# Dilated attention: the steps that merge the three groups moved to other places, and a later load of token differences

## The chip, the cores and the metric

The kernel runs on one core of one Trainium2 chip. The metric is the device time of one execution in microseconds. A core has five engines that each work through their own list of instructions strictly in order: TensorE (PE in the profile, with PEld for loading its stationary operand), VectorE (DVE), ScalarE (ACT), GpSimd (POOL) and SyncE (SP), which in this kernel only issues DMA transfers. Engines wait for each other by semaphores. PE writes to eight PSUM banks; everything else is held in on-chip memory (SBUF) or in device memory.

## The reference, cut to what matters

The whole kernel is one encoder block with three parallel mixers, gates, and two projections. The change concerns the first mixer, attention over three groups of dilated windows, whose outputs are merged with softmax weights over the groups:

```python
for gi, (window, dil) in enumerate(A_GROUPS):          # (128, 1), (512, 4), (2048, 16)
    hs = slice(gi * A_HEADS, (gi + 1) * A_HEADS)       # 8 heads of 64 in each group
    o_g, lse_g = dilated_window_attention(aq[:, :, hs], ak[:, :, hs], av[:, :, hs], window, dil)
    outs.append(o_g)
    lses.append(lse_g)
wts = jax.nn.softmax(jnp.stack(lses, axis=0), axis=0).astype(dt)
oa = jnp.einsum('gbsh,gbshd->bshd', wts, jnp.stack(outs, axis=0)).reshape(b, s, BRANCH_WIDTH)
```

Everything is float32, with 1024 tokens and a width of 1024. Dense products are done with each operand split into a high part (fp32r) and a remainder, and three products (high by high, low by high, high by low).

## The kernel before, in words

**Stages.** The kernel goes through stages one after the other. The change touches dilated attention (about 735 to 1010 us of the profiled span), and the first microseconds of the next stage, which computes gate products with a blocked scheme of seven products (`PRODUCTS`) and needs differences of token blocks ("T2", "T3", "T1", "T4") that an earlier stage left in device memory (`tsd`).

**Items.** Dilated attention is cut into twelve items `(p_, g)`: four pairs of heads, and for each pair the groups 0, 1 and 2. `seq` lists them, in the order (0,0), (0,1), (0,2), (1,0) and so on. `item` (line 1276) returns the pieces of one item for eight token tiles T = 0 to 7:

- `scores(b)`: PE multiplies queries and keys for four token tiles into four PSUM banks (`pss1`, four buffers).
- `soft(T)`: for each of two heads DVE adds the mask and takes the row minimum (L1355), and ACT takes the exponential with a row sum (L1356).
- `trans(T)`: PE transposes the probabilities (L1373, L1382) into a PSUM bank (`pst`, two buffers), and ACT copies them to `app` (L1385).
- `pv(b)`: PE multiplies four tiles' probabilities with the values (L1399) into a bank of the same two-buffer kind, and ACT copies the result to `og` (L1407).
- `stats`: row minima and sums are transposed and written to device memory (`std`).

**The plan.** `plan` (line 1448) lines up the pieces of one item with the tail of the item before it and the head of the next. In each step T stand, in this order: `stats` of the item before (T = 2), `soft(T)`, the merge steps that are due (`combining(T)`), in the last item the token differences (`tokens(T)`), keys for an item two further on (`keys`: in T = 1 a fetch by SP, in T = 5 `k_add`, two additions on POOL, L1274), then `trans(T - 2)` (for T below 2: `trans(T + 6)` of the item before). T = 3 ends with `pv(1)` of the item before joined with `scores(1)` of this one, and T = 7 with `pv(0)` of this one joined with `scores(0)` of the next. `values` (SP loads) follow these two. So `trans(4)` and `trans(5)` come just ahead of `pv(0)`, and `trans(6)`, `trans(7)` are done in the next item.

**Weaving.** `weave` (line 176) mixes these pieces, by their planned cost, with one dense unit for each item: 48 matmuls of 512 columns into two `d` banks, whose results DVE and POOL rotate into the queries `aq` of the item two further on (L1207, L1210, L1211), taken from a list `pend`. In the second half of a unit the next unit's weights are split (`a_split`: ACT `wh`, then DVE `wl`, L105 and L106). In the items (3,1) and (3,2) the units are gates instead (one unit and three units). On DVE, ACT, POOL and SP the order is the order in which the code runs; nothing is reordered later.

**Merging the groups.** When the third group's `pv(1)` of pair p is done (T = 3 of item (p+1, 0)), `ready` puts the steps of `combine` (line 1508) into the list `todo`, and `combining(T)` runs a step when T equals the entry of `STEP_T` (line 1594) that belongs to it. For pairs 0 to 2 the steps are:

- `fetch`: SP loads minima and sums of the three groups from `std` to `cpt` (two DMAs).
- `weights`: seven small DVE operations and a reciprocal, with one ACT exponential between them, give the weights `ceg`.
- `put`: SP writes them to device memory (`wgd`, two DMAs).
- `get`: SP loads them back, spread over 64 partitions each, as three tiles `wgt` (six DMAs of 256 KB).
- three times `weigh(g)`: DVE multiplies `og` of group g by its weights (L1551, 128x1024), and for g = 1, 2 POOL adds it to group 0 (L1553).
- `store`: SP writes the sum to `od`.

Pair 3 is merged in the next stage from a table of its own (`COM`), which the change doesn't touch.

**The last item.** In front of item (3,2) the tiles `wgt` (three), `kraw`, `kswp`, `t1a`, `aq`, `ak` are reused for token differences: eight loads of 256 KB (`load_block`, SP), which are split on ACT and DVE (`split_block`) two at a time in T = 2 to 5 (`tokens`). The tail of that item (`plan(None, ...)`, T = 0 to 3: `trans(6)`, `trans(7)`, `stats`, `pv(1)`) follows, and then the next stage begins with the products A11·B11, A12·B21 and S2·T2.

Of the kernel before, what the change touches and what calls it, by code (L numbers as in the profile page):

```python
# [9 lines left out]
R = mybir.dt.float32r  # L10
# [5 lines left out]
S = 1024  # L16
NT = 8
P = 128
# [32 lines left out]
def block(ctx: ExitStack, tc: tile.TileContext, x, xT, memT, cst, msk, bcst, tabA, gpost,  # L51
# [52 lines left out]
    def split(dst_h, dst_l, src):  # L104
        A.activation(dst_h, src, AF.Copy)  # L105
        V.tensor_tensor(dst_l, src, dst_h.bitcast(F32), op=OP.subtract)  # L106
# [136 lines left out]
    def pool(name, side="left"):  # L243
        p = tc.tile_pool(name=name, bufs=1, side=side, reuse_waits="tile")
        return p, p.__enter__()
# [109 lines left out]
    late = []  # L355
# [823 lines left out]
    abp, ab = pool("ab")  # L1179
    with tc.tile_pool(name="aa", bufs=1, reuse_waits="tile") as aa:  # L1180
# [263 lines left out]
        def joined(*pieces):  # L1444
            pieces = [x for x in pieces if x]
            return (lambda: [fn() for fn, _ in pieces]), JOINED

        def plan(it, pre, nxt):

            out = []  # L1450

            def combining(T):
                while todo and T == STEP_T[-len(todo)]:
                    todo.pop(0)()

            def tokens(T):
                if T >= 2:
                    for nm, k in late[:2]:
                        split_block(nm, k)
                    del late[:2]  # L1460
                if T == 5:
                    token_tiles("T1", [ab.tile([P, S], R, name=f"a{c}", bufs=2) for c in "qk"])
                    load_block("T1", (0, 1))

            def keys(key, T):
                (k_fetch if T == 1 else k_add)(*key)

            def ready():
                if pre and pre["key"][1] == 2:
                    todo.extend(combine(pre["key"][0], [OG.pop((pre["key"][0], x)) for x in range(3)]))  # L1470

            if it and not pre:
                out.append(it["scores"][0])
            for T in range(NT if it else 4):
                if T == 2 and pre:
                    out.append(pre["stats"])
                if it:
                    out.append(it["soft"][T])
                out.append((lambda T=T: combining(T), 0.0))
                if it and not nxt:  # L1480
                    out.append((lambda T=T: tokens(T), 0.0))
                if it and it["ahead"] and T in (1, 5):
                    out.append((lambda T=T: keys(it["ahead"], T), 0.0))
                if T < 2:
                    if pre:
                        out.append(pre["trans"][T + 6])
                elif it:
                    out.append(it["trans"][T - 2])
                if T == 3:
                    out.append(joined(pre and pre["pv"][1], it and it["scores"][1]))  # L1490
                    if it:
                        out.append(it["values"][1])
                    if pre and it:
                        out.append((ready, 0.0))
                if T == 7:
                    out.append(joined(it["pv"][0], nxt and nxt["scores"][0]))
                    if nxt:
                        out.append(nxt["values"][0])
            return out

        def run(pieces):
            for fn, cost in pieces:
                yield cost
                fn()

        OG = {}

        def combine(p_, ogs):

            c = {}  # L1510
            wgt = [None] * 3

            def load(g):
                wgt[g] = (ab if p_ < 3 else cb).tile([P, S], F32, name="wgt", bufs=3 if p_ < 3 else 1)
                for h in range(2):
                    nc.sync.dma_start(wgt[g][h * 64:h * 64 + 64], wgd[p_, h, g:g + 1].to_broadcast([64, S]))

            def fetch():
                c["t"] = cb.tile([P, 3, 2, 16], F32, name="cpt", bufs=1)
                for h in range(2):  # L1520
                    nc.sync.dma_start(c["t"][h * 64:h * 64 + 64], std[p_, h].rearrange("g s (i e) -> i g s e", e=16))

            def weights():
                cpt = c["t"]
                mn = cb.tile([P, 16], F32, name="cmn", bufs=2)
                V.tensor_tensor(mn, cpt[:, 0, 0], cpt[:, 1, 0], op=OP.min)
                V.tensor_tensor(mn, mn, cpt[:, 2, 0], op=OP.min)
                eg = cb.tile([P, 3, 16], F32, name="ceg", bufs=1)
                V.tensor_tensor(eg, cpt[:, :, 0], mn[:, None, :].to_broadcast([P, 3, 16]), op=OP.subtract)
                A.activation(eg, eg, AF.Exp, scale=-1.0)  # L1530
                dn = cb.tile([P, 3, 16], F32, name="cdn", bufs=1)
                V.tensor_tensor(dn, eg, cpt[:, :, 1], op=OP.mult)
                ds_ = cb.tile([P, 16], F32, name="cds", bufs=2)
                V.tensor_tensor(ds_, dn[:, 0], dn[:, 1], op=OP.add)
                V.tensor_tensor(ds_, ds_, dn[:, 2], op=OP.add)
                V.reciprocal(ds_, ds_)
                V.tensor_tensor(eg, eg, ds_[:, None, :].to_broadcast([P, 3, 16]), op=OP.mult)
                c["e"] = eg

            def put():  # L1540
                for h in range(2):
                    nc.sync.dma_start(wgd[p_, h].rearrange("g (i e) -> i g e", e=16), c["e"][h * 64:h * 64 + 64])

            def get():
                for g in range(3):
                    load(g)

            def weigh(g):
                wv = wgt[g].rearrange("p (b a) -> p a b", b=16)
                ogv = ogs[g].rearrange("p (a b) -> p a b", b=16)  # L1550
                V.tensor_tensor(ogv, ogv, wv, op=OP.mult)  # L1551
                if g:
                    G.tensor_tensor(ogs[0], ogs[0], ogs[g], op=OP.add)  # L1553

            def store():
                nc.sync.dma_start(od[0, p_], ogs[0])

            w3 = [lambda g=g: weigh(g) for g in range(3)]
            if p_ < 3:
                return [fetch, weights, put, get] + w3 + [store]  # L1560
            return [fetch, weights, put] + [f for g in range(3) for f in (lambda g=g: load(g), w3[g])] + [store]
# [16 lines left out]
        TB = {}  # L1578

        def token_tiles(nm, tiles):  # L1580
            TB.setdefault(nm, []).extend([t[:, half[x]] for x in range(2)] for t in tiles)

        def load_block(nm, ks=range(4)):
            for k in ks:
                nc.sync.dma_start(TB[nm][k][1].bitcast(F32), tsd[int(nm[1]) - 1, k])

        def split_block(nm, k):
            h, l = TB[nm][k]
            split(h, l, l.bitcast(F32))

        late = []

        todo = []
        STEP_T = (4, 7, 7, 0, 3, 5, 7, 2)
        seq = [(p_, g) for p_ in range(4) for g in range(3)]
        counter = iter(range(len(AU)))
        add_a(*seq[0])
# [18 lines left out]
        for n in range(len(seq)):  # L1616
            if n + 2 < len(seq):
                add_a(*seq[n + 2])
            elif n + 2 == len(seq):
                for j in GATES_A:  # L1620
                    add_ag(*j)
            last = n + 1 == len(seq)
            if last:
                token_tiles("T2", [ab.tile([P, S], R, name="wgt", bufs=3) for k in range(3)])
                token_tiles("T2", [ab.tile([P, S], R, name="kraw")])
                token_tiles("T3", [ab.tile([P, S], R, name="kswp")])
                TB["T3"].append([ab.tile([P, 512], R, name="t1a", bufs=2) for _ in range(2)])
                token_tiles("T3", [ab.tile([P, S], R, name=f"a{c}", bufs=2) for c in "qk"])
                load_block("T2")
                load_block("T3")  # L1630
                late += [("T2", k) for k in range(4)] + [("T3", k) for k in range(4)]
            pieces = plan(items[n], items[n - 1] if n else None, items[n + 1])
            if last:
                pieces += plan(None, items[n], None)
            weave(len(GATES_A) - 1 if last else 1, run(pieces), sum(c for _, c in pieces), 1.0)
# [20 lines left out]
    last = len(pairs) - 1  # L1656
# [82 lines left out]
    steps = [(n, i, f) for n, i in enumerate((2, 0, 1)) for f in range(8)]  # L1739
# [13 lines left out]
    pre = {}  # L1753
# [163 lines left out]
    for T in range(NT):  # L1917
# [7 lines left out]
        for a, b in cuts:  # L1925
            c = slice(a, b)
# [21 lines left out]
        else:  # L1948
# [9 lines left out]
            for h, (a, b) in enumerate(cuts):  # L1958
                c = slice(a, b)
# [131 lines left out]
```

## Time and profile before

| | us |
|---|---|
| runs, median (lowest, highest) | 1453.93 (1451.42, 1454.14) |
| the profiled execution, its own time | 1452.82 |
| the profiled execution, span from first to last instruction | 1450.8 |
| dilated attention within the span | about 735 to 1010 |
| granted TensorE clock, mean over the span | 0.993 |

The rows shown further down come from views of this one profiled execution. A row of the timeline has the start in us from the span's start, the duration in us, the engine, the line of the kernel and the operation, its output and input tiles, shapes, and how many equal instructions follow each other (x); a bracket gives the idle time of the engine before it and what ended it. A row of the busy-time table has the stretch, its length, and the busy time and number of instructions of PE, PEld, DVE, ACT and POOL, then the granted clock of PE (1.00 is full speed), the share of the DMA engines and GB/s. A row of the waits has who waited, for whom, the total in us, how many times, and the longest.

### The profile page before, as it was taken

The numbers are of one execution on the slowest core, as the hardware profiler recorded it, in microseconds if no ns is written. First come the engines' busy times: TensorE is split into PE (matmuls) and PEld (weight loads), VectorE is DVE, ScalarE is ACT, GpSimd is POOL, SyncE is SP. The second block draws the span as 40 slices with busy tenths as digits, with TensorE's granted clock in tenths as the row PEclk, the third lists the DMA queues.
The fourth block names the chain that finished last, engine by engine and source line by source line (L and its number), as shares of the span: only waits on it lengthen the run. The fifth ranks groups of instructions, "written<-read, shape, count | busy, mean of one in ns | idle before, by whom it ended". The sixth has DMA issues, their size and how long they took to land.

```text
span 1450.8 us, 21207 instructions
## 1 busy us (share of the span) xinstructions
PE 1412.4 (97%) x7556; PEld 1137.8 (78%) x7556; DVE 996.3 (69%) x1765; ACT 656.9 (45%) x1423; POOL 507.4 (35%) x390
## 2 busy tenths in 40 slices
PE   8999999999999999999999898989999999999998
PEld 7899986565666888888888777877787887888887
DVE  7765468776763884788866767655877787559643
ACT  6544365665654453322166475646443344223221
POOL 1415504666664001433244343411333331044322
PEclk9999999999999999999999999999999999999999
DMA  6332012232112788444634546363444443767122
GB/s 238 102 117 74 20 62 91 81 105 74 56 50 88 250 264 280 141 167 167 193 95 120 120 117 153 85 174 104 151 135 140 172 175 130 260 212 272 55 88 102
DMA packets 114137, 198.68 MB, mean 137 GB/s; under 512 B 24624, under 2 KB 55408, under 8 KB 114032
## 3 DMA queue, kind: packets, MB, share of 16 engines
q1 hardware_dynamic: 87824, 166.75, 36.4%
q10 hardware_dynamic: 26208, 30.58, 6.0%
q8 instruction: 59, 0.97, 0.3%
q14 instruction: 46, 0.38, 0.1%
HBM read 142.40 MB, written 54.89 MB: 136 GB/s over the span
## 4 chain that ended last, share of the span: by engine, by line
PE 76%; DVE 8%; ACT 5%; issue 4%; DMA 4%; POOL 3%; ACTq 0%; SPq 0%; POOLq 0%; DVEq 0%
PE s L125 16%; PE sc L125 9%; PE d L145 6%; PE d L143 6%; PE d L147 6%; PE s L1059 5%; PE sc L1937 5%; PE ov L761 3%; PE s L1343 2%; PE tr L1399 2%; PE s L745 2%; PE tr L727 2%; PE s L746 2%; PE d L542 2%; PE d L1059 1%
## 5 line engine op out<-in xcount | busy, mean ns | idle before, releaser
L143 PE MATMUL d<-hh,wh 128*128 128x512 f32 x480 | 195.8, 408 | 1.6 <-DVE fth L228 1.6
L147 PE MATMUL d<-hh,wl 128*128 128x512 f32 x480 | 193.6, 403 | 0.0
L145 PE MATMUL d<-hl,wh 128*128 128x512 f32 x480 | 191.8, 400 | 0.0
L752 POOL TENSOR_TENSOR bl<-bl,bp 128x512 f32<-128x512 f32 x96 | 131.4, 1369 | 53.7 <-ACT bp L748 48.2
L105 ACT ACTIVATE wh<-wr 128x512 fp32r<-128x512 f32 (+1 forms) x91 | 68.8, 772 | 141.7 <-PE sc L125 78.4
L125 PE MATMUL sc<-hh,wh 128*128 128x512 f32 x384 | 118.5, 390 | 2.2 <-ACT rs L1694 2.2
L1356 ACT ACTIVATE pra<-pra,sts 128x192 f32<-128x192 f32 (+2 forms) x192 | 84.6, 442 | 76.0 <-DVE sts L1355 75.6
L106 DVE TENSOR_TENSOR wl<-wr,wh 128x512 fp32r<-128x512 f32 (+1 forms) x63 | 77.3, 1245 | 58.2 <-ACT wh L105 58.0
L143 PEld LDWEIGHTS d<-hh,wh 128*128 128x128 f32 x480 | 90.6, 189 | 22.9 <-issue 4.0
L145 PEld LDWEIGHTS d<-hl,wh 128*128 128x128 f32 x480 | 90.6, 189 | 22.3 <-issue 6.5
L147 PEld LDWEIGHTS d<-hh,wl 128*128 128x128 f32 x480 | 90.6, 189 | 21.5 <-issue 4.5
L728 DVE TENSOR_REDUCE bn<-tr 128x1 f32<-128x512 f32 x128 | 86.1, 685 | 17.8 <-PE tr L727 16.4
L748 ACT ACTIVATE bp<-s 128x512 f32<-128x512 f32 x128 | 75.8, 595 | 47.0 <-PE s L746 46.1
L106 DVE TENSOR_TENSOR ch<-sf,ch 128x512 fp32r<-128x512 f32 x68 | 57.9, 852 | 44.5 <-ACT ch L105 44.5
L125 PEld LDWEIGHTS sc<-hh,wh 128*128 128x128 f32 x384 | 72.1, 188 | 17.4 <-issue 2.6
L1664 POOL TENSOR_TENSOR sf<-wr 128x512 f32<-128x512 f32 x22 | 32.0, 1474 | 151.6 <-DVE ch L106 59.5
L105 ACT ACTIVATE ch<-sf 128x512 fp32r<-128x512 f32 x68 | 41.6, 628 | 90.0 <-PE s L125 46.4
L1207 DVE SCALAR_TENSOR_TENSOR t2a<-d,tab 32x512 f32<-32x512 f32 x96 | 66.0, 687 | 22.7 <-PE d L147 20.7
L1868 POOL TENSOR_TENSOR acc<-acc,th 128x1024 f32<-128x1024 f32 x15 | 40.6, 2708 | 111.8 <-DVE th L1867 111.8
L997 POOL TENSOR_TENSOR sf<-wr 128x512 f32<-128x512 f32 x12 | 19.0, 1583 | 167.2 <-DMA wr<-in_wu 109.6
L1211 POOL TENSOR_TENSOR aq<-t1a,t2a 128x512 f32<-128x512 f32 x24 | 45.4, 1893 | 86.8 <-DVE t1a L1210 86.8
L125 PE MATMUL sc<-hl,wh 128*128 128x512 f32 x192 | 74.8, 389 | 0.0
(392 smaller groups left out, 3773.1 us busy)
## 6 DMA issues: line engine op xcount, KB each, us to landing
wr<-in_wu SPq DMA_DIRECT2D x64, 512.0 KB
kd<-kr ACTq DMA_DIRECT2D x48, 256.0 KB
th<-thd SPq DMA_DIRECT2D x24, 512.0 KB
thd<-rs ACTq DMA_DIRECT2D x44, 256.0 KB
g2d<-fth SPq DMA_DIRECT2D x24, 256.0 KB
kraw<-kd SPq DMA_DIRECT2D x12, 512.0 KB
kswp<-kd SPq DMA_DIRECT2D x48, 128.0 KB
wgt<-wgd SPq DMA_DIRECT2D x24, 256.0 KB
```

The source lines that it names most:

```text
L105: A.activation(dst_h, src, AF.Copy)
L106: V.tensor_tensor(dst_l, src, dst_h.bitcast(F32), op=OP.subtract)
L125: PE.matmul(out_ps, a, b, start=i == 0, stop=i == n - 1)
L143: PE.matmul(dst, wh[:, k, :], hh[k][:, t], start=k == 0, stop=False)
L145: PE.matmul(dst, wh[:, k, :], hl[k][:, t], start=False, stop=False)
L147: PE.matmul(dst, wl[:, k, :], hh[k][:, t], start=False, stop=k == 7)
L728: fp["last"] = V.tensor_reduce(st[i]["n"][:, j, c:c + 1], s, axis=AX.X, op=OP.min)
L748: A.activation(pp, s, AF.Exp, scale=-1.0)
L752: G.tensor_tensor(lsum[i % 2], lsum[i % 2], pp, op=OP.add)
L1059: PE.matmul(now[j], a, b, start=k == 0 and q == 0, stop=k == end and q == 2)
L1356: A.activation(src, src, AF.Exp, scale=-1.0, bias=bias, accum_out=sts[:, h, 1, T:T + 1])
L1937: PE.matmul(parts[h], *terms[h][j], start=j == 0, stop=j == 23)
```

## The change

Four things change, all in the stage of dilated attention.

1. `fetch` is no longer in `todo`: it runs at once in `ready` (end of T = 3 of item (p+1, 0)).
2. The other seven steps get new places. Before: `weights` and `put` in T = 7 of item (p+1, 0); `get` in T = 0 and the three `weigh` in T = 3, 5, 7 of item (p+1, 1); `store` in T = 2 of item (p+1, 2). Now: `weights` in T = 5, `put` in T = 6, `get` in T = 7 of item (p+1, 0); `weigh(0)` and `weigh(1)` in T = 4 and 5 of item (p+1, 1); `weigh(2)` in T = 4 and `store` in T = 7 of item (p+1, 2).
3. The tiles for the token differences T2 and T3 are taken and loaded in T = 4 of the last item instead of in front of it.
4. They are split in T = 6 and 7 of the last item and in the first two steps of its tail (two in each), instead of in T = 2 to 5.

```diff
             def tokens(T):
-                if T >= 2:
-                    for nm, k in late[:2]:
-                        split_block(nm, k)
-                    del late[:2]
+                if T == 4:
+                    token_tiles("T2", [ab.tile([P, S], R, name="wgt", bufs=3) for k in range(3)])
+                    token_tiles("T2", [ab.tile([P, S], R, name="kraw")])
+                    token_tiles("T3", [ab.tile([P, S], R, name="kswp")])
+                    TB["T3"].append([ab.tile([P, 512], R, name="t1a", bufs=2) for _ in range(2)])
+                    token_tiles("T3", [ab.tile([P, S], R, name=f"a{c}", bufs=2) for c in "qk"])
+                    load_block("T2")
+                    load_block("T3")
+                    late.extend([("T2", k) for k in range(4)] + [("T3", k) for k in range(4)])
+                if T > 5:
+                    late_split()
                 if T == 5:
                     token_tiles("T1", [ab.tile([P, S], R, name=f"a{c}", bufs=2) for c in "qk"])
                     load_block("T1", (0, 1))
 
+            def late_split():
+                for nm, k in late[:2]:
+                    split_block(nm, k)
+                del late[:2]
+
             def ready():
                 if pre and pre["key"][1] == 2:
-                    todo.extend(combine(pre["key"][0], [OG.pop((pre["key"][0], x)) for x in range(3)]))
+                    fetch, *steps = combine(pre["key"][0], [OG.pop((pre["key"][0], x)) for x in range(3)])
+                    fetch()
+                    todo.extend(steps)
...
                 if it and not nxt:
                     out.append((lambda T=T: tokens(T), 0.0))
+                if not it:
+                    out.append((late_split, 0.0))
...
-        STEP_T = (4, 7, 7, 0, 3, 5, 7, 2)
+        STEP_T = (5, 6, 7, 4, 5, 4, 7)
...
             last = n + 1 == len(seq)
-            if last:
-                token_tiles("T2", [ab.tile([P, S], R, name="wgt", bufs=3) for k in range(3)])
-                token_tiles("T2", [ab.tile([P, S], R, name="kraw")])
-                token_tiles("T3", [ab.tile([P, S], R, name="kswp")])
-                TB["T3"].append([ab.tile([P, 512], R, name="t1a", bufs=2) for _ in range(2)])
-                token_tiles("T3", [ab.tile([P, S], R, name=f"a{c}", bufs=2) for c in "qk"])
-                load_block("T2")
-                load_block("T3")
-                late += [("T2", k) for k in range(4)] + [("T3", k) for k in range(4)]
             pieces = plan(items[n], items[n - 1] if n else None, items[n + 1])
```

No instruction is added or removed. PE's instructions stand in the same order as before; on ACT, DVE, POOL and SP the moved ones stand at their new places between unchanged neighbours.

## Prediction

> **What bounds the kernel now.** I read the busy time of the stage first, then DVE's waits in it, then the timeline around one wait.
>
> ```profile
> 735.00:1020.00 285.00, 270.81 (x2018) 221.19 (x2017) 185.60 (x544) 173.42 (x543) 92.83 (x49) 0.97 0.45 122
> DVE og L1551 <- DMA wgt<-wgd: 18.7, 3, 6.8
> ...
> 750.92 1.81 PE L1343 MATMUL s<-ak,aq 64*128 64x128 f32 x24
> 761.41 1.16 PE L1343 MATMUL s<-ak,aq 64*128 64x128 f32 x16
> 812.63 1.81 PE L1343 MATMUL s<-ak,aq 64*128 64x128 f32 x24
> 829.45 1.16 PE L1343 MATMUL s<-ak,aq 64*128 64x128 f32 x16
> ...
> 815.54 2.00 DVE L1551 TENSOR_TENSOR og<-og,wgt 128x1024 f32<-128x1024 f32 x1 [6.80 <-DMA wgt<-wgd]
> 819.00:820.00 1.00, 0.00 (x0) 0.00 (x0) 0.97 (x5) 0.57 (x3) 0.00 (x0) 1.00 0.99 209
> 820.00:821.00 1.00, 0.16 (x1) 0.16 (x2) 0.97 (x6) 1.00 (x4) 0.00 (x0) 1.00 1.10 172
> 823.00:824.00 1.00, 1.00 (x5) 0.63 (x3) 0.99 (x2) 0.00 (x0) 0.91 (x1) 0.50 0.34 64
> ```
>
> PE is the bound: in the stage it is busy 270.81 of 285.00 us, so 14.2 us are idle. No other engine is near; each matters only where it makes PE stand. Three times, once for each of pairs 0 to 2, DVE stands up to 6.8 us at `weigh(0)` because its weights are still on their way (18.7 us in all). DVE runs in order, so `soft` of four tiles is late, then ACT's exponentials and copies, then PE. The distance from `scores(1)` to the next `scores(0)` shows the price: 10.49 us in item (0,1) without a merge (750.92 to 761.41), 16.82 us in (1,1) with it, 6.3 us more. After the hole at 819 to 820.8 the granted clock drops to 0.50, so part of the price is a slow clock. Over the stage the clock is 0.97 of full: 285.00 x 0.03 = 8.5 us. Idle time and clock together are 14.2 + 8.5 = 22.7 us, which the change could win at most: 1452.82 (the profiled execution's own time) - 22.7 = **1430.1 us** as the base without any stall. That execution lies 1.1 us below the runs' median of 1453.93.
>
> **The change part by part.** What counts is which new place holds up `soft`.
>
> (a) *`fetch` to `get`, items (1,0), (2,0), (3,0).*
>
> ```profile
> 791.96 1.29 SPq L1521 DMA_DIRECT2D cpt<-std  x2
> 792.77 4.10 POOL L1274 TENSOR_TENSOR ak<-kraw,kswp 128x512 f32<-128x512 f32 x2 [4.57 <-DMA avs<-vdr]
> 793.55 0.42 DVE L1355 CUSTOM_DVE_ANT_0 pra<-s,mask 128x256 f32<-128x256 f32 x1
> 794.50:795.00 0.50, 0.50 (x4) 0.41 (x3) 0.47 (x2) 0.50 (x2) 0.50 (x2) 1.00 0.03 3
> 795.34 0.41 DVE L1355 CUSTOM_DVE_ANT_0 pra<-s,mask 128x256 f32<-128x256 f32 x1
> ...
> 799.57 0.44 PE L1399 MATMUL tr<-app,avs 128*64 128x128 f32 x4
> 800.53 0.17 DVE L1526 TENSOR_TENSOR cmn<-cpt 128x16 f32<-128x16 f32 x1
> 802.77 1.37 DVE L1207 SCALAR_TENSOR_TENSOR t2a<-d,tab 32x512 f32<-32x512 f32 x2
> 807.95 3.65 SPq L1516 DMA_DIRECT2D wgt<-wgd  x6
> ...
> 1047.78 1.61 POOL L1664 TENSOR_TENSOR sf<-wr,sf 128x512 f32<-128x512 f32 x1
> 1048.18 1.25 DVE L1526 TENSOR_TENSOR cmn<-cpt 128x16 f32<-128x16 f32 x1
> ```
>
> `weights` moves from 800.53, behind `soft(7)`, to behind `soft(5)`, which ends at 793.98 (a second 0.42 after the one shown): ahead of `soft(6)` at 795.34. `cpt` is asked for at 791.96 and the transfer engines are silent by 794.5, so I put its arrival there. The chain of `weights` takes 2.24 us (800.53 to 802.77). But POOL is then in `k_add` until 796.87. The pair at 1047.78 shows what that does: `cmn`, elsewhere 0.17 us, took 1.25 and ended with POOL's addition. So the chain starts in effect at 796.87 and ends near 799.0; then t2a and t1a (two rotations, 1.3 us) and `soft(6)` at 800.3 in place of 795.34. ACT's copy for `trans(4)` stands behind the exponentials of `soft(6)` and frees the bank of `pv(0)`: 1.8 us from `soft(6)` to `pv(0)` with 192 columns (rows in (b)), 2.1 estimated with 256. `pv(0)` starts at 802.4, not 799.57: **2.8 us x 3 = 8.4**. Without the holding the chain ends at 797.0 and the stall is 0.8.
>
> Gained is that the six loads of `get`, now ahead of the item's other loads in SP's list, are asked for near 801.5 instead of 807.95, and 7.6 us (807.95 to 815.54) bring them in by 809, long before `weigh`. The whole old stall goes. On SP, `put` waits for the chain's end near 799 with only `get` and the item's later loads behind it; these (`avs`, `avp`, `wr`) are asked for later by the 3.65 us that six issues take. The values among them serve `pv(0)` of the next item near 821, so I cost this at nothing; without that cover it would be 3.65 an item.
>
> (b) *`weigh(0)` and `weigh(1)` together, items (1,1), (2,1), (3,1).*
>
> ```profile
> 820.93 2.02 DVE L1551 TENSOR_TENSOR og<-og,wgt 128x1024 f32<-128x1024 f32 x1
> 823.09 2.36 POOL L1553 TENSOR_TENSOR og<-og 128x1024 f32<-128x1024 f32 x1 [13.28 <-DVE og L1551]
> 824.29 0.35 DVE L1355 CUSTOM_DVE_ANT_0 pra<-s,mask 128x192 f32<-128x192 f32 x1
> 825.57 0.47 ACT L1385 ACTIVATE app<-tr 128x384 f32<-128x384 f32 x1
> 826.09 0.69 PE L1399 MATMUL tr<-app,avs 128*64 128x128 f32 x4 [1.95 <-ACT app L1385]
> ...
> 828.88 0.34 DVE L1355 CUSTOM_DVE_ANT_0 pra<-s,mask 128x192 f32<-128x192 f32 x1
> ...
> 755.51 0.35 DVE L1355 CUSTOM_DVE_ANT_0 pra<-s,mask 128x192 f32<-128x192 f32 x1
> 759.51 0.44 PE L1399 MATMUL tr<-app,avs 128*64 128x128 f32 x4
> ```
>
> These rows show the chain: `soft(6)` 824.29, the copy 825.57, `pv(0)` 826.09, 1.80 later. In (0,1), without a merge, `soft(6)` is at 755.51 and `pv(0)` at 759.51; moved by the 61.71 us between the two `scores(1)`, 817.22 and 821.22. Two weighings ahead of it, 2 x 2.02, put `soft(6)` at 821.26 and `pv(0)` at 823.06: 1.8 us late. From the second weighing to the end of `soft(7)` it took 8.5 us (820.93 to 829.4); by the same chain the second half of `scores(0)` loses 0.9 more. **2.8 x 2 = 5.5**; (3,1), whose gate unit has no rotations, 1.0 (0 to 1.5).
>
> (c) *`weigh(2)` in T = 4, POOL's addition behind it, items (1,2), (2,2).* The same place in (0,2):
>
> ```profile
> 772.95 4.30 POOL L1274 TENSOR_TENSOR ak<-kraw,kswp 128x512 f32<-128x512 f32 x2 [6.22 <-PE s L1343]
> 773.01 0.70 DVE L1207 SCALAR_TENSOR_TENSOR t2a<-d,tab 32x512 f32<-32x512 f32 x1
> 775.61 0.28 DVE L1355 CUSTOM_DVE_ANT_0 pra<-s,mask 128x128 f32<-128x128 f32 x1
> 777.18 2.15 POOL L1211 TENSOR_TENSOR aq<-t1a,t2a 128x512 f32<-128x512 f32 x1
> 778.32 2.17 DVE L106 TENSOR_TENSOR wl<-wr,wh 128x512 fp32r<-128x512 f32 x2 [2.21 <-ACT wh L105]
> 780.14 2.01 PE L1343 MATMUL s<-ak,aq 64*128 64x128 f32 x18
> 780.41 0.28 DVE L1355 CUSTOM_DVE_ANT_0 pra<-s,mask 128x128 f32<-128x128 f32 x1
> ```
>
> `weigh(2)` pushes `soft(6)` by 2.0 to 777.6. The addition (2.36) must wait for it, and `k_add`, now queued behind, shifts from 772.95 to 777.5, its halves (2.15 each) reaching to 781.8. DVE's `wl`, two reads of SBUF as well, comes to stand among them; at 778.32 it took 2.17 against POOL's one 2.15. If `wl` gets in between the halves, `soft(7)` ends at 783.5 instead of 780.9; if behind both, 785.6. That bank is needed by the second half of the next `scores(0)`, which ran in one go from 780.14: 2.4 or 4.5 us, I take 3.5. **3.5 x 2 = 7.0**. The Trainium skill, page "SBUF — State Buffer", section "Who interferes with whom", says that whichever of a two-input DVE operation and a GpSimd read starts first keeps a shared port for its whole instruction while the other blocks. Row 1048.18 agrees (1.25 against 0.17); by that rule alone the upper 4.5 would hold and the sum be 2 us higher. In (3,2) no `k_add` follows: nothing.
>
> (d) *Token differences.* Eight loads and eight splits move later.
>
> ```profile
> 981.99 1.14 ACT L105 ACTIVATE wgt<-wgt 128x512 fp32r<-128x512 f32 x2
> ...
> 1008.75 0.38 ACT L1385 ACTIVATE app<-tr 128x256 f32<-128x256 f32 x1 [0.38 <-PE tr L1382]
> 1009.85 0.88 PE L1399 MATMUL tr<-app,avs 128*64 128x128 f32 x12
> ```
>
> Two splits cost ACT 1.14. T = 7 and two steps of the tail put six ahead of the tail's copies: 3 x 1.14 = 3.4 behind 1008.75, so the copy ends at 1012.2 and `pv(1)` starts there instead of 1009.85: **2.4** (0 if ACT's idle time ahead of them takes them, 4 if loads are late too). S2·T2, which reads them, is the third product, behind two others.
>
> (e) *Clock.* New idle time is 8.4 + 5.5 + 1.0 + 7.0 + 2.4 = **24.3 us** (22 to 26.5), in nine places, most of 2 to 3.5 us.
>
> ```profile
> 1224.00:1228.00 4.00, 1.80 (x9) 1.20 (x8) 2.68 (x4) 1.44 (x2) 0.00 (x0) 1.00 0.83 289
> ```
>
> Above, 1.84 us of idle time brought half clock for 6.7 us, a price of 3.3; here 2.2 us of idle time cost nothing. So between 0 and 24.3 x 8.5 / 14.2 = 14.5, the old proportion. The pieces are like both rows; I take the middle, **7.3**. (The Trainium skill, "TensorE: Matmul & The Clock Gate", section "What's actually happening", lets the clock fall only after an idle window of about 3.4 us. By that rule the term would be 0 and the time 1454; the row at 823 shows a drop after 1.84, and the measurement decides.)
>
> Sum: 1430.1 + 24.3 + 7.3 = **1462** (rounded), 8 us slower than the median.
>
> **The rivals.**
>
> *Cover suffices: faster.* Only the holding by POOL and the bank's chain make the new stalls. If `cmn` slips through while `k_add` runs and `wl` too, (a) is 3 x 0.8 = 2.4, (b) 2 x 1.8 = 3.7 with (3,1) at 0.5, (c) 0.2, (d) 2.4: 9.2, at full clock: 1430.1 + 9.2 = 1439. For it: 800.53 shows `cmn` at 0.17, and DVE is 65% busy in the stage. Against it: the row at 1048.18.
>
> *Same stalls, no clock loss:* 1430.1 + 22.1 = 1452, no change. For it the row at 1224; against it the one at 823.
>
> *The wait moves to `cpt`.* `weights` now stands right behind its load, and `soft(6)` queues behind it. The only sure bound of the landing is 800.53, when it was used: chain to 802.8, 3.7 us later than in (a), 3 x 3.7 = 11 more: 1473 (it decides from a landing past 797). Against it: silence at 794.5.
>
> *It doesn't do what it says:* `wgt` would have to take over 15 us from 801.5 to be late again; it took 7.6. Time as before, 1454.
>
> **How the numbers follow.** Forecast 0.58, its own range 1455 to 1471; cover suffices 0.25; no clock loss 0.10; the wait moves 0.05; no effect 0.02. A measurement of this kernel can tell about 0.2% (2.9 us) from no change. Faster: the 0.25, 0.03 of the case without clock loss: 0.28. Same: 0.07 of that case and 0.02 of no effect, 0.09. Slower: 0.58 + 0.05 = 0.63. The range must reach the faster case, 1438, and ends at 1471.
>
> **What would show it.** Right: no wait of `og` L1551 for `wgt`; in the (p+1,0) items `cmn` over 1 us, ending with a `k_add`, and `pv(0)` behind an idle PE of 2 to 3 us with `app` as releaser; `k_add` of (1,2) behind `og` on POOL; the clock under 1.00 after these. Wrong: `cmn` at 0.17 and `pv(0)` within 1 us; PE idle under 10 us in the stage with the clock near 1.00 (faster), or DVE waiting for `cpt` (the wait moved).

## The result, and the profile after

| | before | after |
|---|---|---|
| runs beside each other, median (us) | 1452.84 | 1463.3 |
| ratio to before, 95% interval | | 1.0074 [1.0056, 1.0091] |
| span of the profiled execution (us) | 1450.8 | 1462.4 |

The change made the kernel slower by 10.5 us; 1462 was forecast. First the busy time of the same stretch of the changed kernel, and its waits in the stage (DVE's, then PE's):

```profile
735.00:1020.00 285.00, 262.68 (x1963) 213.26 (x1961) 188.10 (x532) 166.54 (x532) 90.99 (x47) 0.98 0.42 118
DVE cmn L1542 <- DMA cpt<-std: 2.9, 3, 1.2
PE tr L1399 <- ACT app L1385: 12.1, 6, 2.7
PE s L1343 <- DVE sts L1355: 8.8, 5, 3.7
```

The wait of `og` for `wgt`, 18.7 us before, is gone. In its place PE waits at `pv(0)` (L1399) six times for a copy and at `scores(0)` (L1343) for `soft`, and does 8 us less of its work in the same stretch. Where, the distances between groups of `scores` tell, since PE's order is the same in both kernels. The rows around (a) in pair 0, first the changed kernel's PE and DVE, then POOL:

```profile
791.22 1.96 PE L1343 MATMUL s<-ak,aq 64*128 64x256 f32 x18
803.13 0.70 PE L1399 MATMUL tr<-app,avs 128*64 128x128 f32 x4 [2.67 <-ACT app L1385]
806.64 1.81 PE L1343 MATMUL s<-ak,aq 64*128 64x128 f32 x24
...
796.05 1.69 DVE L1542 TENSOR_TENSOR cmn<-cpt 128x16 f32<-128x16 f32 x1 [1.24 <-DMA cpt<-std]
797.77 0.17 DVE L1543 TENSOR_TENSOR cmn<-cmn,cpt 128x16 f32<-128x16 f32 x1
799.68 0.69 DVE L1207 SCALAR_TENSOR_TENSOR t2a<-d,tab 32x512 f32<-32x512 f32 x1
800.99 0.41 DVE L1355 CUSTOM_DVE_ANT_0 pra<-s,mask 128x256 f32<-128x256 f32 x1
...
793.60 4.10 POOL L1274 TENSOR_TENSOR ak<-kraw,kswp 128x512 f32<-128x512 f32 x2 [4.62 <-DMA avs<-vdr]
```

`cmn` takes 1.69 us and ends at 797.74, with POOL's `k_add` (793.60 + 4.10 = 797.70); the next operation of the same kind takes 0.17. From there the chain, the two rotations, `soft(6)` at 800.99 and `pv(0)` at 803.13 follow as forecast, 2.67 us behind an idle PE. The distance 791.22 to 806.64 is 15.42 us; before it was 790.39 to 801.47 = 11.08.

The same for (c) in pair 0, POOL, DVE and PE of the changed kernel:

```profile
844.91 2.39 POOL L1569 TENSOR_TENSOR og<-og 128x1024 f32<-128x1024 f32 x1 [7.44 <-DVE og L1567]
847.27 4.19 POOL L1274 TENSOR_TENSOR ak<-kraw,kswp 128x512 f32<-128x512 f32 x2
851.42 2.55 POOL L1211 TENSOR_TENSOR aq<-t1a,t2a 128x512 f32<-128x512 f32 x1
...
849.40 5.12 DVE L106 TENSOR_TENSOR wl<-wr,wh 128x512 fp32r<-128x512 f32 x2 [1.53 <-ACT wh L105]
854.45 0.28 DVE L1355 CUSTOM_DVE_ANT_0 pra<-s,mask 128x128 f32<-128x128 f32 x1
...
854.79 2.28 PE L1343 MATMUL s<-ak,aq 64*128 64x256 f32 x8 [3.72 <-DVE sts L1355]
```

POOL's three jobs stand end to end until 853.97, and the two `wl` beside them take 5.12 us (1.28 where POOL is idle, the row at 800.75 of e8 below). `soft(7)` and the second half of `scores(0)` wait, 3.72 us.

The whole stage, as time above the undisturbed distance, by place. The distance runs from the first matmul of one `scores` group to that of a later one; undisturbed it is, in the kernel before, 11.07 in (a); 10.49 + 10.20 in (b) with the half item behind it; 8.52 + 10.28 in (c); the tail (d) took 22.52 from its last `scores` to the first product of the next stage. The two places of (b) in the last pair are set against 10.49 and 20.24.

| us above the undisturbed distance | (a) | behind (a) | (b) | (c) | (d) | sum |
|---|---|---|---|---|---|---|
| before | 0 | 0 | 21.6 | 0 | 0 | 21.6 |
| after | 9.2 | 0 | 7.1 | 12.9 | 1.9 | 31.2 |
| e1, `weights` in T = 7 | 0 | 0 | 9.5 | 14.0 | 1.9 | 25.4 |
| e2, addition of `weigh(2)` in T = 6 | 9.7 | 1.2 | 7.1 | 10.1 | 1.9 | 30.0 |
| e3, `weigh(1)` in T = 7 | 8.6 | 2.1 | 6.9 | 11.6 | 1.9 | 31.1 |
| e4, before with late token differences | 0 | 0 | 19.1 | 0 | 1.9 | 20.9 |
| e5, `k_add` of group 0 in the next item | 3.5 | 9.9 | 7.1 | 14.2 | 1.9 | 36.6 |
| e6, no addition of group 2 | 9.3 | 0 | 7.1 | 5.3 | 1.9 | 23.6 |
| e7, steps in DVE's gaps | 0.7 | 0 | 3.2 | 0 | 1.9 | 5.8 |
| e8, e7 and later splits in the tail | 0.7 | 0 | 3.2 | 0 | 1.0 | 4.9 |

After minus before is 9.6 of the 11.6 us between the two spans. The other 2.0 lie in work that the change leaves alone: 0.8 ahead of the first changed place and 1.1 behind the stage, where the changed kernel has a further 3.4 us at half clock (from 1236.55) that the kernel before doesn't have. Differences of 1 to 2 us between runs at a place that an edit leaves alone are mostly half clock that the same stall brought in one run and not in another (last section).

### The profile page after: what moved, and what is told of

Same layout as the page of the kernel before. It is cut to its first block, busy times and chain, and to the rows that moved or that the text cites. A ratio compares the mean times of both kernels' runs of the same rounds, so it can differ in the third digit from the quotient of the medians.

```text
span 1462.4 us, 21210 instructions
## 1 busy us (share of the span) xinstructions
PE 1415.4 (97%) x7556; PEld 1137.6 (78%) x7556; DVE 1007.4 (69%) x1765; ACT 657.0 (45%) x1423; POOL 508.3 (35%) x390
## 4 chain that ended last, share of the span: by engine, by line
PE 81%; DVE 7%; ACT 4%; issue 3%; DMA 2%; POOL 2%; SPq 1%; ACTq 0%; POOLq 0%; DVEq 0%
PE s L125 22%; PE sc L125 9%; PE s L1059 6%; PE d L143 6%; PE d L145 6%; PE d L147 6%; PE sc L1944 5%; PE ov L761 3%; PE tr L1399 2%; PE s L1343 2%; PE d L1059 2%; PE s L745 2%; PE s L746 2%; PE tr L727 2%; DVE wl L106 1%
## 5 line engine op out<-in xcount | busy, mean ns | idle before, releaser
L106 DVE TENSOR_TENSOR wl<-wr,wh 128x512 fp32r<-128x512 f32 (+1 forms) x63 | 84.3, 1356 | 53.9 <-ACT wh L105 53.7
L997 POOL TENSOR_TENSOR sf<-wr 128x512 f32<-128x512 f32 x12 | 19.4, 1615 | 167.2 <-DMA wr<-in_wu 109.8
L125 PE MATMUL s<-hh,ch 128*128 128x512 f32 x224 | 73.7, 390 | 0.2 <-ACT ch L105 0.2
```

The source lines that it names most:

```text
L125: PE.matmul(out_ps, a, b, start=i == 0, stop=i == n - 1)
```

## Experiments

The ratios are to the kernel before, run on the same chip.

**e1: undo (a) alone.**

```diff
-        STEP_T = (5, 6, 7, 4, 5, 4, 7)
+        STEP_T = (7, 7, 0, 4, 5, 4, 7)
```

> The changed kernel, but weights and put in T = 7 (behind soft(7)) and get in T = 0 of the next item. Theory: the chain of weights ahead of soft(6) is what makes PE stand before pv(0) of the (p+1,0) items; without it the distance between scores(1) and the next scores(0) falls back by 4.3 + 2.4 + 2.5 us, so 9.2 us less than the changed kernel: 1454, about 1.001 of the kernel before. Rival: the earlier load is needed for weigh(0) in T = 4, which now waits for wgt again by 3 us or more in each of three items: 1461 or more. In the trace: no PE idle time over 0.5 us before pv(0) near 803, and either no wait of og for wgt (theory) or three of them (rival).

1455.87 us, ratio 1.0023 [1.0010, 1.0035], 1.9 us above the theory's number. (a) fell from 9.2 to 0 over the three pairs, as the theory has it. But the rival had a share: `wgt` was late again twice, by 2.3 us in all, and the stalls at `pv(0)` of (1,1) and (2,1) grew from 1.58 and 1.60 to 2.76 and 2.60. DVE and PE of this run, in (1,1):

```profile
815.34 2.02 DVE L1567 TENSOR_TENSOR og<-og,wgt 128x1024 f32<-128x1024 f32 x1 [1.21 <-DMA wgt<-wgd]
823.84 0.69 PE L1399 MATMUL tr<-app,avs 128*64 128x128 f32 x4 [2.76 <-ACT app L1385]
```

So the early load is worth something; what costs in (a) is the place of `weights`.

**e2: POOL's addition behind `k_add`.**

```diff
-                if g:
-                    G.tensor_tensor(ogs[0], ogs[0], ogs[g], op=OP.add)
+                if g and (p_ == 3 or g == 1):
+                    add(g)
+
+            def add(g):
+                G.tensor_tensor(ogs[0], ogs[0], ogs[g], op=OP.add)
...
-                return [fetch, weights, put, get] + w3 + [store]
+                return [fetch, weights, put, get] + w3 + [lambda: add(2), store]
...
-        STEP_T = (5, 6, 7, 4, 5, 4, 7)
+        STEP_T = (5, 6, 7, 4, 5, 4, 6, 7)
```

> The changed kernel, but POOL's addition that belongs to weigh(2) is issued in T = 6, behind k_add, while DVE's multiplication stays in T = 4. Theory (POOL's queue): k_add runs early again, the two wl behind soft(6) take under 2.6 us instead of 5.1, and both stalls of 3.7 us in the second half of scores(0) go with the clock they cost, 7.0 + 5.7 = 12.7 us: 1450.6, 0.998 of the kernel before. Rival (DVE's two us ahead of soft(6) alone are to blame): at least 2 us of each stall stay, 1457 or more.

1463.11 us, ratio 1.0064 [1.0042, 1.0085]: a miss. (c) only fell from 12.9 to 10.1. POOL and DVE in pair 1:

```profile
913.41 6.14 POOL L1274 TENSOR_TENSOR ak<-kraw,kswp 128x512 f32<-128x512 f32 x2 [5.11 <-PE s L1343]
919.46 2.16 POOL L1211 TENSOR_TENSOR aq<-t1a,t2a 128x512 f32<-128x512 f32 x1
921.54 2.83 POOL L1572 TENSOR_TENSOR og<-og 128x1024 f32<-128x1024 f32 x1
...
913.35 2.03 DVE L1567 TENSOR_TENSOR og<-og,wgt 128x1024 f32<-128x1024 f32 x1
920.02 4.90 DVE L106 TENSOR_TENSOR wl<-wr,wh 128x512 fp32r<-128x512 f32 x2 [1.53 <-ACT wh L105]
```

`k_add` did start early, but took 6.14 us, since `weigh(2)` on DVE now held it for its two us; and the rotation (919.46) and the moved addition (921.54) came to stand beside `wl` where `k_add` had been. The two `wl` took 4.90, and PE's stall in `scores(0)` is 3.44 us, nearly the old 3.69. In pair 0 three waits of 0.50, 1.19 and 0.69 stand in place of the one of 3.72. So it is not the order of POOL's queue that decides, but whatever POOL runs while DVE reads two operands from SBUF. The time fits the rival (DVE's two us alone) as well; e6 tells the two apart.

**e3: `weigh(1)` behind `soft(7)`.**

```diff
-        STEP_T = (5, 6, 7, 4, 5, 4, 7)
+        STEP_T = (5, 6, 7, 4, 7, 4, 7)
```

> The changed kernel, but weigh(1) in T = 7, behind soft(7). Theory: two weighings ahead of soft(6) make the three stalls of 1.5 to 1.6 us before pv(0) of the (p+1,1) items; they go, 1.7 + 1.7 + 1.5 = 4.9 us less: 1458.4, 1.004 of the kernel before. Rival (the delay only moves behind soft(7), where the next rotations and the copies of trans(6) wait): 1 us or more comes back in each, 1461 to 1463.

1459.71 us, ratio 1.0056 [1.0034, 1.0079]: between the two numbers, and not to be told apart from the changed kernel (1.0074). The stall before `pv(0)` went in (1,1) and (2,1), where the distance is 10.49 again; but it came back behind, as the rival says, by a wait that neither had named. ACT, then PE:

```profile
830.58 1.08 ACT L1407 ACTIVATE og<-tr 128x512 f32<-128x512 f32 x1 [3.31 <-POOL og L1569]
831.71 0.55 PE L1373 MATMUL tr<-cs,pra 128*128 128x128 f32 x3 [1.30 <-ACT og L1407]
```

ACT's copy of `pv` into `og` stands 3.31 us for POOL's addition, which comes late after the late `weigh(1)`. ACT works in order, so PE's transposes wait for it.

**e4: the token differences alone.** The kernel before, with `tokens`, `late_split` and the piece in the tail as in the change, and the old `STEP_T`.

```diff
             def tokens(T):
-                if T >= 2:
-                    for nm, k in late[:2]:
-                        split_block(nm, k)
-                    del late[:2]
+                if T == 4:
...
+                    load_block("T2")
+                    load_block("T3")
...
+                if T > 5:
+                    late_split()
...
+                if not it:
+                    out.append((late_split, 0.0))
...
-            if last:
...
```

> The kernel before with the token differences alone moved (loads in T = 4 of the last item, splits in T = 6, 7 and the first two steps of the tail); all merge steps at their old places. Theory as recorded: six splits ahead of the tail's copies cost 2.4 us, 1455.2, 1.0016 of the kernel before; by the changed kernel's trace (distance from the last scores to the first product 43.55 to 44.63 us) 1.1 us: 1453.9, 1.0007. Rival: this part costs nothing or gains, and the tail's loss in the changed kernel is due to weigh(2) in the last item: 1452.8 or less.

1454.76 us, ratio 1.0019 [1.0005, 1.0034], by the ratio 2.8 us more (0.7 to 4.9). The tail took 985.82 to 1010.20 = 24.38 us in place of 22.52, the same 1.9 as in the changed kernel: the part is a loss by itself, and `weigh(2)` in the last item has no share in it.

**e5: is it POOL that holds `cmn`?**

```diff
-                if it and it["ahead"] and T in (1, 5):
+                if it and it["ahead"] and T in ((1,) if it["key"][1] == 0 else (1, 5)):
                     out.append((lambda T=T: keys(it["ahead"], T), 0.0))
+                if T == 0 and pre and pre["ahead"] and pre["key"][1] == 0:
+                    out.append((lambda: k_add(*pre["ahead"]), 0.0))
```

> The changed kernel, but the two additions k_add that belong to the items of group 0 are issued at T = 0 of the next item, far from the weights. Theory (POOL's running addition holds the first minimum of the chain): cmn takes about 0.17 us instead of 1.7, soft(6) comes 1.5 us sooner, and the stalls of 2.7, 2.4 and 2.4 us before pv(0) shrink to 0.9 to 1.3 each: 4 to 6 us less than the changed kernel with the clock, 1457.5 to 1459.5. Rival (the landing of cpt and the length of the chain make the stall): cmn may be short, but waits for cpt longer and PE's stalls stay above 2 us: 1462 to 1463.

1469.16 us, ratio 1.0129 [1.0113, 1.0145]. On the question asked, the theory held: DVE's chain, then PE:

```profile
796.68 0.17 DVE L1544 TENSOR_TENSOR cmn<-cpt 128x16 f32<-128x16 f32 x1 [1.53 <-DMA cpt<-std]
802.76 4.39 DVE L106 TENSOR_TENSOR wl<-wr,wh 128x512 fp32r<-128x512 f32 x2 [1.88 <-ACT wh L105]
802.26 0.44 PE L1399 MATMUL tr<-app,avs 128*64 128x128 f32 x4 [1.45 <-ACT app L1385]
807.49 0.72 PE L1343 MATMUL s<-ak,aq 64*128 64x128 f32 x5 [2.29 <-DVE sts L1355]
```

`cmn` takes 0.17 us, and the stalls before `pv(0)` are 1.45, 0.93 and 0.94 instead of 2.67, 2.38 and 2.37. So POOL's holding is 4.1 of the 7.4 us; the other 3.3 stay without it, with DVE waiting up to 1.53 us for `cpt` and then working through the chain. The time, though, was forecast 10 us too low: POOL started `k_add` as soon as it was free, at 802.27, and so right beside the two `wl`, which took 4.39 us. A stall of 2.3 us in `scores(0)` follows in each pair (9.9 us behind (a)). The same collision, moved from `cmn` to `wl`, costs more than it did.

**e6: one addition less on POOL.**

```diff
-                if g:
+                if g == 1 or g and p_ == 3:
                     G.tensor_tensor(ogs[0], ogs[0], ogs[g], op=OP.add)
```

> The changed kernel without POOL's addition of group 2 for pairs 0 to 2 (left out, so od lacks that part); DVE's multiplication stays in T = 4. Theory (POOL's adds beside it hold wl): with one addition less on POOL the two wl take under 2.6 us instead of 5.1, and the stalls of 3.7 us in scores(0) fall under 1 us: 11 to 12.7 us less, 1450.6 to 1452.3. Rival (DVE's own two us ahead of soft(6) make it): stalls of 2 us or more stay, 1457 or more.

This kernel leaves out POOL's addition of group 2. 1458.28 us (1454.49 to 1460.41; the profiled execution 1455.97), ratio 1.0054 [1.0038, 1.0071]. By its median the time lies where the rival put it. The trace decides otherwise: no wait in (c) is longer than 1.27 us, where the rival has 2 or more. In the profiled execution (c) fell from 12.9 to 5.3: 7.6 us, not the 11 to 12.7 of the theory. The median fell by less still, and why is not shown. DVE and PE in both pairs:

```profile
841.96 3.86 DVE L1567 TENSOR_TENSOR og<-og,wgt 128x1024 f32<-128x1024 f32 x1
850.46 1.47 DVE L106 TENSOR_TENSOR wl<-wr,wh 128x512 fp32r<-128x512 f32 x2 [1.52 <-ACT wh L105]
...
918.97 2.74 DVE L106 TENSOR_TENSOR wl<-wr,wh 128x512 fp32r<-128x512 f32 x2 [1.53 <-ACT wh L105]
```

The `wl` are short again, 1.47 and 2.74 us, so the larger half of (c) is POOL beside `wl`. The rest is `weigh(2)` itself: in pair 0 `k_add` had started at 841.82, just before it, and it took 3.86 us instead of 2.0, which pushes `soft(6)`. In pair 1 it stretched `k_add` to 6.12, so that POOL's rotation behind that came to stand beside `wl` (the 2.74). Of the 5.3 us 1.7 are clock: 3.4 us at half clock follow the waits of pair 0.

**e7 and e8: a version from these readings.** `weights` goes behind `soft(6)`, into the 2.7 us in which DVE waited for ACT's `wh` in the kernel before. `weigh(0)` and `weigh(2)` go to T = 3, ahead of DVE's waits for PE (in the changed kernel 3.56 us before the rotation at 815.84 and 1.76 before `soft(4)` at 818.98). `weigh(1)` goes to T = 4, so that only one stands between `soft(4)` and `soft(6)`, and POOL's additions end before `wl`.

```diff
-        STEP_T = (5, 6, 7, 4, 5, 4, 7)
+        STEP_T = (6, 6, 7, 3, 4, 3, 7)
```

and for e8 besides

```diff
-                if not it:
+                if not it and T > 1:
                     out.append((late_split, 0.0))
```

> The steps of the changed kernel put into gaps of DVE: weights and put in T = 6, get in T = 7, weigh(0) and weigh(1) in T = 3 and 4 of item (p+1,1), weigh(2) in T = 3 of item (p+1,2). Theory: DVE waits 1.9 to 2.7 us for ACT behind soft(6) and 1.4 to 1.7 us for PE ahead of soft(4), so each step costs PE at most 1 us there, and wgt is in time: residuals of 1.5 for (a), 3 for (b), 1 for (c), 1.1 for the tail on a base of 1463.3 - 30.2 = 1433, so 1440, 0.991 of the kernel before. Rival (any two us more on DVE in an item cost PE two, wherever they stand): weigh alone costs 9 x 2 us, 1451 or more.

> As the run before, and in the tail the splits of T3 stand in its third and fourth step instead of the first two, behind ACT's copies for pv(1). Theory (splits ahead of the copies make the tail's two waits of 0.8 and 0.5 us): both go, 1 us less than the run before, 1439. Rival (the tail is bound by something else, or the splits then come too late for the product S3 T3): no gain, or 1 us worse.

e7: 1437.88 us, ratio 0.9914 [0.9901, 0.9927]. e8: 1436.22 us, ratio 0.9904 [0.9890, 0.9917]. Both beat the two kernels, and both came a little under the numbers expected (1440 and 1439). The stage of e8, DVE's chain and PE in (1,0), and the tail:

```profile
735.00:1020.00 285.00, 280.04 (x2082) 228.31 (x2081) 211.68 (x561) 180.79 (x554) 99.68 (x53) 1.00 0.47 131
797.15 1.97 DVE L1543 TENSOR_TENSOR cmn<-cmn,cpt 128x16 f32<-128x16 f32 x1
800.75 1.28 DVE L106 TENSOR_TENSOR wl<-wr,wh 128x512 fp32r<-128x512 f32 x2
800.18 0.44 PE L1399 MATMUL tr<-app,avs 128*64 128x128 f32 x4 [0.36 <-ACT app L1385]
...
990.75 0.44 PE L1382 MATMUL tr<-cs,pra 128*128 128x128 f32 x2 [0.80 <-ACT app L1385]
993.35 1.09 PE L1399 MATMUL tr<-app,avs 128*64 128x128 f32 x16
```

The chain is still held (1.97 us for the second minimum), but in a gap: `wl` starts at 800.75, right behind the chain, `pv(0)` waits 0.36, and the distance is 0.4 us above the undisturbed one. The clock is 1.00 through the stage. In the tail one of two waits is gone and the tail is 0.9 us shorter; the other, 0.80, is left, since T = 7 of the item has its splits ahead of a copy too. The intervals of e7 and e8 overlap, so this last gain is read from the trace, not from the runs.

## Why the prediction was right

**The base.** 1430.1 from idle time and clock put the old stalls at 22.7 us; by the distances they were 21.6, so the base should have been about 1431.2.

**(a)** 8.4 us of idle time forecast, 2.67 + 2.38 + 2.37 = 7.4 measured. The cause given, POOL holding the first minimum, is shown by e5 for 4.1 us of the 7.4; the prediction put the rest, the stall without the holding, at 0.8 a pair, and e5 has 0.9 to 1.45. One input was off: `cpt` was put at 794.5, or 795.3 with the 0.83 us by which the changed run is behind at `scores(1)`; DVE waited for it until 796.05. Here that cost nothing, because POOL held on until 797.70; in e5, without the holding, it is part of the 1.45. The rival in which the wait moves to `cpt` thus had its wait (2.9 us in all) without its price.

**(b)** 5.5 + 1.0 forecast; the stalls are 1.58 + 0.59, 1.60 + 0.59 and 1.48, together 5.8. That two weighings stand between `soft(4)` and `soft(6)` is the cause: with the second behind `soft(7)` (e3), or the first ahead of `soft(4)` (e7), the first distance in (1,1) and (2,1) is 10.48 to 10.49. What e3 adds is that the second can't simply go behind `soft(7)`. In (3,1) 1.3 us stay in e7, and what holds them was not looked into.

**(c)** 7.0 forecast, 3.72 + 3.69 = 7.4 measured. The place and the holding were right: without the addition the `wl` of pair 0 fall from 5.12 to 1.47 (e6). The way to it was half right. The step had `k_add`, pushed back in POOL's queue, as the thing in the way; e2 took that push away, and in pair 1 3.44 of 3.69 us stayed, because any POOL operation beside `wl` that reads SBUF does it, and DVE's weighing holds up POOL as well.

**(d)** 2.4 forecast, 1.9 measured by the tail's distance, alone in e4 and in the changed kernel. The splits were the cause, but the delay was forecast for the start of `pv(1)`, and PE waits at two earlier places, 0.80 at `trans(6)` and 0.54 at `stats`. ACT's splits ahead of a copy in the tail of the changed kernel, then PE, which waits for it:

```profile
1015.35 0.62 ACT L105 ACTIVATE wgt<-wgt 128x512 fp32r<-128x512 f32 x1
1015.87 0.61 ACT L105 ACTIVATE kraw<-kraw 128x512 fp32r<-128x512 f32 x1
1016.39 0.36 ACT L1385 ACTIVATE app<-tr 128x256 f32<-128x256 f32 x1
1016.81 0.44 PE L1382 MATMUL tr<-cs,pra 128*128 128x128 f32 x2 [0.80 <-ACT app L1385]
```

**(e)** 7.3 forecast. Half clock was granted behind three of the stalls:

```profile
803.00:804.00 1.00, 0.86 (x8) 0.87 (x10) 0.37 (x1) 1.00 (x3) 0.14 (x1) 0.53 0.85 283
804.00:805.00 1.00, 1.00 (x14) 1.00 (x12) 1.00 (x3) 0.12 (x1) 0.00 (x0) 0.50 1.04 250
806.00:807.00 1.00, 1.00 (x13) 0.77 (x11) 0.87 (x2) 1.00 (x4) 0.00 (x0) 0.76 0.99 238
...
854.00:855.00 1.00, 0.21 (x2) 0.22 (x3) 0.97 (x6) 0.17 (x1) 0.00 (x0) 0.63 0.00 0
861.00:862.00 1.00, 1.00 (x6) 0.76 (x5) 0.35 (x4) 0.75 (x4) 1.00 (x1) 0.96 0.28 74
...
929.00:930.00 1.00, 1.00 (x7) 0.89 (x7) 0.99 (x2) 1.00 (x6) 0.00 (x0) 0.68 0.54 111
932.00:933.00 1.00, 1.00 (x4) 0.77 (x4) 0.97 (x5) 0.00 (x0) 0.00 (x0) 0.62 1.02 373
```

What a row's clock lacks to 1.00, doubled, is its time at half speed: 0.94 + 1 + 1 + 0.48 = 3.4 us behind 2.67 of idle time, 0.74 + 6 + 0.08 = 6.8 behind 3.72, 0.64 + 1 + 1 + 0.76 = 3.4 behind 3.69 (the seconds not shown are at 0.50). Half of their sum, 13.6, is lost: 6.8. Behind the others (2.38, 2.37, 1.60 and shorter) nothing was lost. That the middle of 0 to 14.5 came so close is partly luck: in e3 the first stall is nearly the same, 2.65 us, and cost no clock (distance 13.79 instead of 15.42).

**The sum.** 24.3 + 7.3 = 31.6 forecast, 31.2 measured; the base was 1.1 too low. The agreement is better than its parts: the waits of PE over 0.5 us at these places add up to 22.0 instead of 24.3, with the clock 28.8, and the 2.4 us to 31.2 lie in shorter waits that were not followed up. The rival in which the cover suffices fell with (a) and (c), the one without clock loss with these rows. That rival's sum also took 22.1 for the stalls, where the prediction's own are 24.3; with those it gives 1454, as under (e).

## What to carry to other kernels

A wait that is removed by starting its cause earlier is only gained in full if the earlier place is a gap of that engine: here the same steps cost 31 us in one set of places and 6 in another, with the same instructions. Look for the places where the engine waits anyway (here DVE behind `soft(6)` and ahead of `soft(4)`), and put moved work there, one piece each. Where two engines hold each other, look at pairs that run at the same time, not at the order of one queue: twice here a remedy that moved POOL's work away from one DVE operation put it beside another.

## What the runs showed of the hardware

The holding goes both ways. DVE's `weigh` of 2.0 us stretched POOL's two `k_add` from 4.3 to 6.14 us (e2), and a `k_add` that had just started stretched `weigh` to 3.86 (e6). The Trainium skill, page "SBUF — State Buffer", section "Who interferes with whom", says that a DVE instruction with two inputs in SBUF contends with a GpSimd instruction that reads SBUF, that the shared ports are an exclusive lock, and that issue order decides who blocks. Both rows agree: `weigh` issued first in e2 (913.35) and took its 2.03 us, and `k_add` issued first in e6 (841.82).

Time at half clock came in pieces of 3.4, 6.8 and 3.4 us. The Trainium skill, page "TensorE: Matmul & The Clock Gate", section "What's actually happening", has a free-running window of about 3.4 us, and the pieces agree with one and two of these. So do their starts: by the rows under (e) these are 804 - 0.94 = 803.06, 855 - 0.74 = 854.26 and 930 - 0.64 = 929.36, and so 51.20 and 75.10 us apart, 15 and 22 times 3.41. The clock changed on a fixed grid, wherever the stalls lay.

That a drop needs an idle window of that length, as the same section of the Trainium skill has it, doesn't agree with the drops behind 2.67 us in the changed kernel and 1.84 us in the kernel before. The steps of the grid ahead of the three drops, and then the steps with most of the stalls of 2.38 and 2.37 us, which kept the clock:

```profile
799.65:803.06 3.41, 0.82 (x6) 0.51 (x4) 2.07 (x6) 1.55 (x6) 1.84 (x1) 1.00 0.12 22
850.85:854.26 3.41, 0.21 (x2) 0.00 (x0) 3.41 (x2) 0.00 (x0) 3.12 (x2) 1.00 0.31 87
925.94:929.35 3.41, 0.57 (x5) 0.55 (x7) 3.38 (x7) 0.53 (x3) 2.02 (x1) 1.00 0.16 44
874.74:878.15 3.41, 1.73 (x10) 1.19 (x8) 2.62 (x9) 0.93 (x4) 1.22 (x1) 1.00 0.07 7
949.83:953.24 3.41, 1.67 (x30) 1.67 (x32) 1.53 (x6) 2.62 (x7) 1.76 (x1) 1.00 0.61 145
```

PE was busy for 0.82, 0.21 and 0.57 us of the 3.41 ahead of the drops, and for 1.73 and 1.67 where the clock stayed. Over the ten traces of this case, from 735 to 1420 us, every step at full clock in which PE was busy for 1.32 us or less was followed by half clock (24 steps), and none in which it was busy for 1.79 or more; of the eleven between (1.45 to 1.73), five were. So what counts here is how much PE works in one step of the grid, and a stall of 2 to 3 us is paid for when it falls into one step and may go free when it lies across two.

The length of a stall doesn't decide by itself, which is read from e3, whose stalls at the three places of (a) are 2.65, 2.32 and 2.31 us. The windows behind the first and the second:

```profile
802.00:806.00 4.00, 3.62 (x56) 3.35 (x56) 3.08 (x8) 2.83 (x9) 0.39 (x1) 1.00 0.92 236
876.00:878.00 2.00, 2.00 (x19) 1.67 (x17) 1.96 (x7) 1.30 (x5) 0.00 (x0) 0.50 1.02 242
```

The longer stall kept the full clock and the shorter lost it, the other way round than in the changed kernel (2.67 lost it, 2.38 kept it). In the step of the grid with most of the longer stall PE was busy for 1.79 us, in that with the shorter for 1.31. No run here moved a stall against the grid on purpose.
